# Seven products in place of eight for three of the eight k pairs of gate and up, with the FFN's work in a written-out order

## The chip, the cores and the metric

One core of a Trainium2 chip runs the whole program. The metric is the device time of one execution in microseconds, and the time of a kernel is the median of its runs. All data are float32. One core has a matrix engine (PE, with its weight loads shown as PEld), a vector engine (DVE), a scalar engine (ACT), GpSimd (POOL) and SyncE (SP), which issues most of the transfers.

## The reference

One decoder layer with 256 tokens, D = 2048 channels and a hidden width of 5632. A gated mixer comes first and is the same in both kernels. The change touches the second half of the layer:

```python
def _swiglu(h, w_gate, w_up, w_down):
    return (jax.nn.silu(h @ w_gate) * (h @ w_up)) @ w_down
...
        h = h + _swiglu(_rmsnorm(h, norm_ffn[l]), w_gate[l], w_up[l], w_down[l])
    return _rmsnorm(h, norm_final)
```

## The kernel before, in words

Every matmul operand is held as two rounded parts, hi and lo, so one product of a 128-row weight tile with a block of tokens takes three matmuls: hi by hi, hi by lo, lo by hi (lines 216 to 218 in the token-stationary form "A"). Weights come from DRAM in tiles of 1 MB (`raw`, line 165, three buffers, issued from SP). Each `raw` is split in two halves of 128x1024 elements: ACT casts a half to `hi` (line 175), then DVE subtracts to get `lo` (line 177). There are five pairs of hi/lo buffers, so a split runs some two tiles ahead of PE and then waits for PE to free a buffer.

The work is a list of blocks that `run_blocks` walks. The last stages are four blocks of the mixer's output projection (`out_evac`, lines 702 to 745), then eleven times a gate block and an up block of 512 hidden columns (`ffn_gate_evac`, `ffn_up_evac`), then four blocks of the down projection. In a gate or up block PE goes over 16 k tiles in eight chunks of two; for each chunk it makes the products of both token halves (n = 0, 1). Gate ends in two banks, which ACT reads with silu (line 764); up ends in two banks, which DVE multiplies with that (line 770); the product is transposed on PE (line 777) and split into `hs` (lines 781, 782), which stays in SBUF until the down projection reads it. `out_evac` also makes `y2s` (the normed-gain input of gate and up, split) and the sums of squares, from which `rms` (line 732) makes `r2`, the factor per token.

Tile places the instructions on each engine by priority; `issue_after` and the work queues (`gla_w_`, `conv_w_`) move small work between chunks. Each engine then goes through its own instructions in a fixed order.

A k pair below is two neighbouring k tiles, p = 0 to 7, with gate's and up's 512 columns of one hidden block.

Of the kernel before, what the change touches and what calls it, by code (L numbers as in the profile page):

```python
# [26 lines left out]
NA = 60  # L27
# [7 lines left out]
def trunk(ctx: ExitStack, tc, xT, par, convw, ws, wal2, nfin, out):  # L35
    nc = tc.nc
    cpool = ctx.enter_context(tc.tile_pool(name="cpool", bufs=1))
    apool = ctx.enter_context(tc.tile_pool(name="apool", bufs=NA))
    tpool = ctx.enter_context(tc.tile_pool(name="tpool", bufs=8))
    wpool = ctx.enter_context(tc.tile_pool(name="wpool", bufs=LOOK + 1))  # L40
    pacc = ctx.enter_context(tc.tile_pool(name="pacc", bufs=8, space=bass.MemoryType.PSUM))
# [108 lines left out]
    def load_next():  # L150
        i = nload[0]
        if i >= len(loads):
            return
# [24 lines left out]
        for x in gs:  # L178
            XU.append(atile([P, 2 * T], F32R, "xu"))
            with tc.issue_after(order["a"]), tc.issue_after(order["v"]):  # L180
                split(XU[-1], x)
        staged[i] = (hi, lo)

    def run_blocks():
# [11 lines left out]
        for b in blocks:  # L196
# [38 lines left out]
            group = LOOK if b is blocks[-1] else 1  # L235
            cs = list(range(nch))
            while cs:
                now = cs[:1] if len(cs) > group else cs
                cs = cs[len(now):]
                while nload[0] < len(loads) and nload[0] <= b["first"] + now[0] + LOOK:  # L240
                    load_next()
                for n in range(nt):
                    for c in now:
                        part(c, n)
                for c in now:
                    del staged[b["first"] + c]
                    pump(b["budget"])
# [70 lines left out]
    def x_scaled(k):  # L318
        def f():
            s = atile([P, 2 * T], F32R, "xs")  # L320
# [362 lines left out]
    def pw_evac(blk):  # L683
        def f(n, a):
# [6 lines left out]
            MG[i] = atile([P, 2 * T], F32R, "mgs")  # L691
# [10 lines left out]
    def out_evac(blk):  # L702
        def f(n, a):
# [6 lines left out]
            y = ttile("y2")  # L710
# [4 lines left out]
            if i % 2 == 1:  # L715
                q = atile([P, 2, T], s="hq")
# [6 lines left out]
            if i == 15:  # L723
                def fold():
                    fo = ttile("hf")
                    v.tensor_tensor(fo, sums["h"][:, 0, :], sums["h"][:, 1, :], op=ALU.add)
                    sums["f"] = fo

                def rms():
                    m = misc()  # L730
                    for h in range(2):
                        pe.matmul(m[:, h:h + 1], lhsT=sums["f"][:, h * P:(h + 1) * P], rhs=ones[:, 0:1],
                                  start=True, stop=True)
                    s = cpool.tile([P, 2], F32, tag="r2s", name="r2s")
                    sc.activation(s, m[:, 0:2], AF.Sqrt, bias=eps6)
                    v.reciprocal(r2, s)
                gla_w_.add(0.0, fold)
                gla_w_.add(0.0, rms, 2)
                gla_w_.mark("rstd2")
                for th in range(2):  # L740
                    for nb in range(4):
                        gla_w_.add(0.0, transp(th, nb), 1)
# [16 lines left out]

    def ffn_gate_evac(blk):  # L760
        def f(n, a):
            gla_w_.drain("rstd2")
            GT[n] = tpool.tile([P, NB], F32, tag="gt", name=nm("gt"), bufs=3)
            sc.activation(GT[n], a, AF.Silu, scale=r2[:, n:n + 1])
        return f

    def ffn_up_evac(blk):
        def f(n, a):
            hd = GT[n]
            v.scalar_tensor_tensor(hd, in0=a, scalar=r2[:, n:n + 1], in1=GT[n], op0=ALU.mult, op1=ALU.mult)  # L770
            hs = HS[blk, n] = [atile([P, NB], F32R, "hs") for _ in range(2)]
            st = {}

            def turn():
                st["m"] = m = misc()
                for j in range(4):
                    pe.transpose(m[:, j * P:(j + 1) * P], hd[:, j * P:(j + 1) * P], ident)  # L777

            def cut():
                m = st["m"]  # L780
                sc.copy(hs[0], m)
                v.tensor_tensor(hs[1], m, hs[0].bitcast(F32), op=ALU.subtract)
            gla_w_.add(0.0, turn, 1)
            gla_w_.add(0.0, cut, 1)
            gla_w_.mark(("hs", blk, n))
        return f

    NFT = {}
    HX = []

    def down_before():
        gla_w_.drain(("hs", 10, 1))
        for i in range(HT):
            j = slice(i % 4 * P, (i % 4 + 1) * P)
            HX.append([[t[:, j] for t in HS[i // 4, n]] for n in range(2)])
        for nb in range(4):
            NFT[nb] = atile([P, NB], s="nf")
            nc.sync.dma_start(NFT[nb], nfin[nb * NB:(nb + 1) * NB].partition_broadcast(P))

    def down_evac(nb):  # L800
        def f(n, a):
            h = HTK[n, nb]
            last = nb == 3
            for p, q in ((0, 256), (256, 512)) if last else ((0, 512),):
                v.tensor_tensor(h[:, p:q], a[:, p:q], h[:, p:q], op=ALU.add)
                sq = atile([P, NB], s="dq")
                c = nb + p // 256
                sc.activation(sq[:, p:q], h[:, p:q], AF.Square, accum_out=ss[:, n, c:c + 1])
            if not last:
                v.tensor_tensor(h, h, NFT[nb], op=ALU.mult)  # L810
                if nb == 2 and n == 1:
                    with tc.issue_after(order["a"]):
                        sc.activation(dummy, eps6, AF.Sqrt)
                return
            s1 = cpool.tile([P, 1], F32, tag=f"s1{n}", name=nm("s1"))
            v.reduce_sum(s1, ss[:, n, :], axis=mybir.AxisListType.X)
            s2 = cpool.tile([P, 1], F32, tag=f"s2{n}", name=nm("s2"))
            sc.activation(s2, s1, AF.Sqrt, scale=1.0 / D, bias=eps6)
            s3 = cpool.tile([P, 1], F32, tag=f"s3{n}", name=nm("s3"))
            v.reciprocal(s3, s2)  # L820
            for m in (0, 1, 3, 2):
                o = atile([P, NB], s="fin")
# [54 lines left out]
    for blk in range(11):  # L877
        add_block(NB, KT, "A", lambda: Y2, ffn_gate_evac(blk), budget=0.01)
        add_block(NB, KT, "A", lambda: Y2, ffn_up_evac(blk), budget=0.01)
    for nb in range(4):  # L880
        add_block(NB, HT, "A", lambda: HX, down_evac(nb),
                  before=down_before if nb == 0 else None, budget=0.0)
    run_blocks()


# [57 lines left out]
```

## Time and profile before

| what | value |
|---|---|
| median of three runs | 1681.61 us (1681.47 to 1683.62) |
| the profiled execution's own time | 1683.09 us |
| its span, first to last instruction | 1681.4 us |
| PE busy | 1664.9 us, 8526 matmuls |
| DVE busy | 1150.5 us |
| ACT busy | 857.1 us |
| moved by DMA | 316.35 MB, mean 188 GB/s |

The profiled execution spends 1.7 us outside its span and is 1.5 us above the median. Busy time of PE counts pipelined matmuls, so a PE that is busy all the time may still be slowed inside a stretch. Busy time of DVE and ACT leaves out the time in which the next instruction of the queue waits for another engine.

### The profile page before, as it was taken

Reading aid. Unit: us, or ns where it says so; the run is one execution under the profiler, and the core shown is the slowest. Engines: PE = TensorE matmul, PEld = TensorE weight load, DVE = VectorE, ACT = ScalarE, POOL = GpSimd, SP = SyncE. Lnnn points to the kernel's source line nnn. Section 1 sums busy time; section 2 is a strip of 40 time slices with the busy share of each in tenths; the row PEclk is TensorE's granted clock in tenths of the full one; section 3 lists DMA queues with packets and bytes.
Section 4 is the critical chain, followed back from the end, with each engine's and each line's share of the span. In section 5 each row is a group of like instructions: output and inputs, shape, how many; then the busy total and the mean of one; then the engine's idle time right before and its main releaser. Section 6 shows DMA issues by size and latency. Waiting matters only on the chain.

```text
span 1681.4 us, 21671 instructions
## 1 busy us (share of the span) xinstructions
PE 1664.9 (99%) x8526; PEld 1414.0 (84%) x8526; DVE 1150.5 (68%) x1725; ACT 857.1 (51%) x1161; POOL 4.5 (0%) x10
## 2 busy tenths in 40 slices
PE   9999999999999999999999999999999999999997
PEld 7888888888888888888888888888888888888886
DVE  7898999888888899886777544444444444444453
ACT  6654444666766654584555644444444444444343
POOL 0000000000000000000000000000000000000000
PEclk9999999999999999999999999999999999999999
DMA  8555555555445455545555555555555545655553
GB/s 294 191 198 179 191 185 190 186 183 178 169 172 176 165 187 177 198 177 201 181 217 200 191 188 178 195 178 191 185 191 184 196 180 189 211 198 185 194 200 100
DMA packets 48405, 316.35 MB, mean 188 GB/s; under 512 B 5392, under 2 KB 6672, under 8 KB 11312
## 3 DMA queue, kind: packets, MB, share of 16 engines
q1 hardware_dynamic: 48160, 314.91, 52.7%
q8 instruction: 66, 1.08, 0.3%
q14 instruction: 35, 0.29, 0.0%
q10 hardware_dynamic: 144, 0.07, 0.0%
HBM read 312.86 MB, written 2.10 MB: 187 GB/s over the span
## 4 chain that ended last, share of the span: by engine, by line
PE 97%; DVE 1%; ACT 1%; DMA 1%; issue 0%; ACTq 0%
PE acc L224 31%; PE acc L225 16%; PE acc L216 15%; PE acc L218 15%; PE acc L217 15%; DVE lo L177 1%; ACT hi L175 1%; PE m L777 1%; DVE gt L770 0%; PE m L583 0%; DMA raw<-in_weights_dram 0%; PE m L498 0%; DMA pr<-in_par_dram 0%; PE m L620 0%; PE m L621 0%; PE m L752 0%
## 5 line engine op out<-in xcount | busy, mean ns | idle before, releaser
L177 DVE TENSOR_TENSOR lo<-raw,hi 128x1024 fp32r<-128x1024 f32 (+1 forms) x590 | 717.5, 1217 | 487.5 <-ACT hi L175 485.5
L175 ACT CAST hi<-raw 128x1024 fp32r<-128x1024 f32 (+1 forms) x590 | 617.2, 1047 | 753.1 <-PE acc L218 424.4
L224 PE MATMUL acc<-xs,hi 128*128 128x512 f32 x1280 | 452.4, 398 | 0.0
L225 PE MATMUL acc<-xs,lo 128*128 128x256 f32 x1280 | 359.0, 280 | 0.0
L224 PEld LDWEIGHTS acc<-xs,hi 128*128 128x128 f32 x1280 | 240.3, 188 | 57.8 <-ACT hi L175 0.3
L216 PE MATMUL acc<-hi,y2s 128*128 128x512 f32 x704 | 276.5, 393 | 0.0
L218 PE MATMUL acc<-hi,y2s 128*128 128x512 f32 x704 | 274.3, 390 | 0.0
L217 PE MATMUL acc<-lo,y2s 128*128 128x512 f32 x704 | 274.0, 389 | 0.0
L225 PEld LDWEIGHTS acc<-xs,lo 128*128 128x128 f32 x1280 | 241.8, 189 | 0.1
L380 DVE SCALAR_TENSOR_TENSOR yc<-u,cw,yc 128x255 f32<-128x255 f32 (+14 forms) x480 | 200.1, 466 | 0.1
L218 PEld LDWEIGHTS acc<-hi,y2s 128*128 128x128 f32 x704 | 132.1, 188 | 27.8
L217 PEld LDWEIGHTS acc<-lo,y2s 128*128 128x128 f32 x704 | 132.3, 188 | 26.8
L216 PEld LDWEIGHTS acc<-hi,y2s 128*128 128x128 f32 x704 | 132.2, 188 | 26.6
L216 PE MATMUL acc<-hi,hs 128*128 128x512 f32 x352 | 137.0, 389 | 0.0
L218 PE MATMUL acc<-hi,hs 128*128 128x512 f32 x352 | 136.9, 389 | 0.0
L217 PE MATMUL acc<-lo,hs 128*128 128x512 f32 x352 | 136.9, 389 | 0.0
L224 PE MATMUL acc<-xu,hi 128*128 128x512 f32 x256 | 91.1, 400 | 2.9 <-DVE xu L89 2.9
L224 PE MATMUL acc<-ogs,hi 128*128 128x512 f32 x256 | 89.9, 395 | 0.0
L224 PE MATMUL acc<-us,hi 128*128 128x512 f32 x256 | 88.8, 391 | 0.0
L224 PE MATMUL acc<-mgs,hi 128*128 128x512 f32 x256 | 88.8, 391 | 0.0
L218 PEld LDWEIGHTS acc<-hi,hs 128*128 128x128 f32 x352 | 66.1, 188 | 13.8
L216 PEld LDWEIGHTS acc<-hi,hs 128*128 128x128 f32 x352 | 66.1, 188 | 13.7
(181 smaller groups left out, 1661.3 us busy)
## 6 DMA issues: line engine op xcount, KB each, us to landing
raw<-in_weights_dram SPq DMA_DIRECT2D x289, 1024.0 KB, 4.8
raw<-in_weights_dram SPq DMA_DIRECT2D x8, 256.0 KB, 4.8
raw<-in_weights_dram SPq DMA_DIRECT2D x4, 512.0 KB, 6.5
xr<-in_xT_dram SPq DMA_DIRECT2D x8, 256.0 KB, 5.4
out_dram<-fin SPq DMA_DIRECT2D x8, 256.0 KB, 3.1
x<-in_xT_dram SPq DMA_DIRECT2D x8, 128.0 KB, 4.9
x<-in_xT_dram SPq DMA_DIRECT2D x4, 256.0 KB, 6.8
nf<-in_norm_final_dram SPq DMA_DIRECT2D x4, 256.0 KB, 6.4
```

The costliest lines, as they stand in the source:

```text
L175: order["a"] = sc.copy(fl(hi), r).ins
L177: order["v"] = v.tensor_tensor(fl(lo), r, fl(hi).bitcast(F32), op=ALU.subtract).ins
L216: pe.matmul(a, lhsT=xh, rhs=hi[:, kk, :], start=st, stop=False)
L217: pe.matmul(a, lhsT=xh, rhs=lo[:, kk, :], start=False, stop=False)
L218: last = pe.matmul(a, lhsT=xl, rhs=hi[:, kk, :], start=False, stop=en)
L224: pe.matmul(a, lhsT=wh, rhs=x, start=st, stop=False)
L225: last = pe.matmul(a[:, T:2 * T], lhsT=wl, rhs=xh, start=False, stop=en)
L380: v.scalar_tensor_tensor(y[:, d:T], in0=u_tile(i)[:, 0:T - d], scalar=cw[:, i, CW - 1 - d:CW - d], in1=y[:, d:T], op0=ALU.mult, op1=ALU.add)
L777: pe.transpose(m[:, j * P:(j + 1) * P], hd[:, j * P:(j + 1) * P], ident)
```

## The change

For three of the eight k pairs (p = 2, 5, 7, the list `SEVEN`) the 2x2 block product (two token halves by two k tiles, two k tiles by gate and up) is made with seven products of tiles and sums of tiles in place of eight products; the seven go to seven banks. The other five pairs make eight products into four of these banks (two for the difference of the token halves). The sums of weight tiles are made on DVE as each tile arrives (`t13`, `t2`, `t4`) and split like the others; the sums of token tiles are made once, in `out_evac` (`token_sums`). The seven banks are combined by DVE at a block's end. The FFN is recorded in a written-out order (`keep_in_program_order`), with two running estimates `vt["d"]` and `vt["p"]` that say where the recording puts DVE's and PE's small work. A step is one k pair, with one 1 MB `raw` in two transfers of 512 KB. The split products of hidden blocks 0 to 8 go to DRAM from POOL's queue (`hsd`, 36 transfers of 256 KB) and are loaded again from SP during the first nine steps of the down projection (`hr`, 36 of 256 KB). The down projection takes blocks 9 and 10 first, and makes two blocks of 512 output columns and both token halves at once. SBUF is divided anew: `pers` (16 tiles) holds what lives long, and `apool` and `tpool` give their place to `fpool` and `xpool` when the output projection begins.

```diff
+NPERS = 16
+NF = 38
+NX = 6
+SEVEN = (2, 5, 7)
...
+    def token_sums(p, y):
+        if p in SEVEN:
+            f = atile([P, 4, P], s="sf")
+            v.tensor_tensor(f[:, 0], y[:, 0, H1], y[:, 1, H1], op=ALU.subtract)
+            v.tensor_tensor(f[:, 1], f[:, 0], y[:, 0, H0], op=ALU.subtract)
+            v.tensor_tensor(f[:, 2], y[:, 0, H0], y[:, 0, H1], op=ALU.subtract)
+            v.tensor_tensor(f[:, 3], y[:, 1, H0], f[:, 1], op=ALU.add)
+            SY[p] = [atile([P, 4, P], F32R, "sy") for _ in range(2)]
+            hi, lo = SY[p]
+        else:
+            f = atile([P, 2, P], s="df")
+            v.tensor_tensor(f, y[:, :, H0], y[:, :, H1], op=ALU.subtract)
+            DY[p] = atile([P, 2, 2, P], F32R, "dy")
+            hi, lo = DY[p][:, 0], DY[p][:, 1]
+        sc.copy(hi, f)
+        v.tensor_tensor(lo, f, hi.bitcast(F32), op=ALU.subtract)
+    HORDER = [9, 10] + list(range(9))
...
+        def split_of(src, key):
+            def f():
+                hi, lo = w[key] = wt("hi"), wt("lo")
+                cast(hi, src())
+                sub(lo, src(), hi)
+            return f
+        if kind != "S":
+            ops.append((1.22, split_of(lambda: w["raw"][:, h], h)))
+            return ops
+        def t13():
+            raw = w["raw"]
+            t = w["t"] = xt("t13", F32)
+            fl = raw.rearrange("p a k n -> p (a k) n")
+            kp(v.tensor_tensor(t, fl[:, 0::3], raw[:, 1, 0:1].broadcast_to([P, 2, NB]), op=ALU.add))
+        def s13():
+            hi, lo = w["t13"] = xt("th"), xt("tl")
+            cast(hi, w["t"])
+            sub(lo, w["t"], hi)
+        def t2():
+            raw = w["raw"]
+            kp(v.tensor_tensor(raw[:, 1, 0], w["t"][:, 1], raw[:, 0, 0], op=ALU.add))
+        def t4():
+            raw = w["raw"]
+            kp(v.tensor_tensor(w["t"][:, 0], raw[:, 1, 0], raw[:, 0, 1], op=ALU.add))
+        def s4():
+            t = w["t4"] = xt("t4")
+            cast(t[:, 0], w["t"][:, 0])
+            sub(t[:, 1], w["t"][:, 0], t[:, 0])
+            del w["t"]
+        if h == 0:
+            return ops + [(1.22, split_of(lambda: w["raw"][:, 0], 0)), (1.22, t13), (1.22, s13)]
+        return [(0.66, t2), (1.22, split_of(lambda: w["raw"][:, 1], 1)), (0.66, t4), (0.66, s4)]
...
+        if kind == "P":
+            dd = [[DY[p][:, i, j] for i in range(2)] for j in range(2)]
+            return [(2, [(y_op(k0 + j, 0), half(0, j)) for j in range(2)]),
+                    (4, [(y_op(k0 + j, 1), half(0, j)) for j in range(2)]),
+                    (5, [(y_op(k0 + j, 1), half(1, j)) for j in range(2)]),
+                    (3, [(dd[j], half(1, j)) for j in range(2)])]
+        s = [[t[:, j] for t in SY[p]] for j in range(4)]
+        t4 = [w["t4"][:, 0], w["t4"][:, 1]]
+        return [(1, [(y_op(k0, 0), half(0, 0))]),
+                (6, [(s[1], half(1, 0))]),
+                (7, [(s[2], half("t13", 1))]),
+                (2, [(y_op(k1, 0), half(0, 1))]),
+                (4, [(y_op(k1, 1), t4)]),
+                (5, [(s[0], half("t13", 0))]),
+                (3, [(s[3], half(1, 1))])]
...
+        def b1(a):
+            kp(sc.copy(new("s"), a))
+        def b6(a):
+            tt(new("u2"), a, e["s"])
+        def b7(a):
+            tt(new("u3"), a, e["u2"])
+        def b2(a):
+            tt(e["s"], a, e["s"])
+            silu(e["s"], 0)
+        def b4(a):
+            tt(new("g"), a, e["u3"])
+            silu(e["g"], 1)
+        def b5(a):
+            tt(e["u3"], a, e["u3"], ALU.subtract)
+            tt(e["u2"], a, e["u2"], ALU.subtract)
...
+            kp(v.scalar_tensor_tensor(x, in0=x, scalar=r2[:, n:n + 1], in1=e[g], op0=ALU.mult, op1=ALU.mult))
+            back(blk, n, x)
+        def b3(a):
+            tt(e["u2"], a, e["u2"])
...
+        def cut(m):
+            hi, lo = HSV[blk, n] = ptile(F32R, "hsh"), ptile(F32R, "hsl")
+            cast(hi, m)
+            sub(lo, m, hi)
+            if blk not in HORDER[:2]:
...
+                    nc.gpsimd.dma_start(d[z], q.bitcast(F32))
+        turn(vt["p"] + 1.5, t)
...
+            for z, q in enumerate((hi, lo)):
+                kp(nc.sync.dma_start(q.bitcast(F32), HSD[blk, n][z]))
...
+        for r, (f, c) in enumerate([(h2_norm, 0.25)] + [(h2_turn(th, nb), 0.45) for th in range(2) for nb in range(4)]):
+            turns.append((3.0 + 4.0 * r, c, f))
...
+                if p < 9:
+                    reload(HORDER[2 + p])
```

**DVE and ACT, one pair with seven products.** Before, in the middle of an up block, DVE has one subtraction per half tile, and ACT one cast per half tile (`hs` is the split of the block's gated product):

```order
L177 TENSOR_TENSOR lo_10025<-raw_10022,hi_10024 128x1024
L782 TENSOR_TENSOR hs_9973<-m_10017,hs_9972 128x512
L177 TENSOR_TENSOR lo_10043<-raw_10022,hi_10042 128x1024
L177 TENSOR_TENSOR lo_10061<-raw_10058,hi_10060 128x1024
L177 TENSOR_TENSOR lo_10077<-raw_10058,hi_10076 128x1024
```

In the changed kernel DVE has for the pairs p = 6 and p = 7 of a block (`t_1859` is the sum tile t13, `th` its cast, `t_1864` the split of the sum t4):

```order
L808 TENSOR_TENSOR lo_9986<-raw_9982,hi_9985 128x1024
L808 TENSOR_TENSOR lo_9999<-raw_9982,hi_9998 128x1024
L808 TENSOR_TENSOR lo_10009<-raw_10005,hi_10008 128x1024
L842 TENSOR_TENSOR t_1859_10018<-raw_10005 128x1024
L808 TENSOR_TENSOR tl_10027<-t_1859_10018,th_10026 128x1024
L851 TENSOR_TENSOR raw_10005<-t_1859_10018,raw_10005 128x512
L808 TENSOR_TENSOR lo_10041<-raw_10005,hi_10040 128x1024
L855 TENSOR_TENSOR t_1859_10018<-raw_10005 128x512
L808 TENSOR_TENSOR t_1864_10051<-t_1859_10018,t_1864_10051 128x512
```

and ACT has for them:

```order
L805 CAST hi_9998<-raw_9982 128x1024
L805 CAST hi_10008<-raw_10005 128x1024
L805 CAST th_10026<-t_1859_10018 128x1024
L805 CAST hi_10040<-raw_10005 128x1024
L805 CAST t_1864_10051<-t_1859_10018 128x512
L805 CAST hi_10063<-raw_10060 128x1024
```

Three of a pair's casts (`th`, `hi_10040`, `t_1864`) read what DVE has written just before, and the DVE instruction that follows reads that cast.

**PE, the first gate block.** Before, the two matmuls for `r2` (line 732) stand in the fifth chunk, behind 55 matmuls of the block:

```order
L216 MATMUL acc_9332<-hi_9328,y2s_9058 128x512
L217 MATMUL acc_9332<-lo_9329,y2s_9058 128x512
L218 MATMUL acc_9332<-hi_9328,y2s_9058 128x512
L216 MATMUL acc_9339<-hi_9328,y2s_9044 128x512
L732 MATMUL m_9362<-ones,hf_9324 128x1 x2
```

In the changed kernel they stand behind the third of the first pair's four groups (18 matmuls after the first of gate and up):

```order
L1139 MATMUL m_9399<-hi_9258,y2s_8620 128x512
L1140 MATMUL m_9399<-lo_9259,y2s_8620 128x512
L1141 MATMUL m_9399<-hi_9258,y2s_8620 128x512
L1034 MATMUL m_9406<-ones,hf_9383 128x1 x2
L1139 MATMUL m_9411<-hi_9258,dy_8625 128x512
```

They moved forward; `hf` is the last thing that `out_evac` makes.

**SP, the end of gate and up.** Before, SP issues one 1 MB tile after the other, with the four loads of the final norm's factor among them:

```order
L165 DMA raw_12732<-in_weights_dram 128x2048
L165 DMA raw_12766<-in_weights_dram 128x2048
L798 DMA nf_12688<-in_norm_final_dram 128x512
L798 DMA nf_12690<-in_norm_final_dram 128x512
L798 DMA nf_12692<-in_norm_final_dram 128x512
L798 DMA nf_12694<-in_norm_final_dram 128x512
L165 DMA raw_12800<-in_weights_dram 128x2048
```

In the changed kernel four loads of a block's stored products stand ahead of each tile, nine times (the first here):

```order
L823 DMA raw_13238<-in_weights_dram 128x1024 x2
L1116 DMA nf_13269<-in_norm_final_dram 128x512 x2
L1116 DMA nf_13272<-in_norm_final_dram 128x512 x2
L1028 DMA hr_13275<-hsd_9854 128x512
L1028 DMA hr_13276<-hsd_9854 128x512
L1028 DMA hr_13279<-hsd_9841 128x512
L1028 DMA hr_13280<-hsd_9841 128x512
L823 DMA raw_13320<-in_weights_dram 128x1024 x2
```

The queue now moves twice the bytes per step during those nine steps.

## Rows read from the trace of the kernel before

**Rows 1.** The page: busy times, and the chain that ended last by engine.
```profile
PE 1664.9 (99%) x8526; PEld 1414.0 (84%) x8526; DVE 1150.5 (68%) x1725; ACT 857.1 (51%) x1161; POOL 4.5 (0%) x10
...
PE 97%; DVE 1%; ACT 1%; DMA 1%; issue 0%; ACTq 0%
```

**Rows 2.** Busy time by stretch: us, engines' busy (count), granted clock, DMA share, GB/s.
```profile
933.00:1433.30 500.30, 496.38 (x2239) 407.89 (x2238) 249.69 (x239) 221.14 (x240) 0.00 (x0) 1.00 0.52 185
1023.50:1068.50 45.00, 44.65 (x201) 36.75 (x200) 22.13 (x20) 19.17 (x20) 0.00 (x0) 1.00 0.53 187
1433.30:1672.50 239.20, 239.20 (x1058) 198.14 (x1056) 113.24 (x104) 96.04 (x106) 0.00 (x0) 1.00 0.51 182
```

**Rows 3.** Groups of one gate and up block (1068.5 to 1113.5): busy, mean ns | idle before.
```profile
L177 DVE TENSOR_TENSOR lo<-raw,hi 128x1024 fp32r<-128x1024 f32 x16 | 19.6, 1225 | 22.9 <-ACT hi L175 22.9
L175 ACT CAST hi<-raw 128x1024 fp32r<-128x1024 f32 x16 | 16.9, 1053 | 24.9 <-PE acc L218 24.9
...
L770 DVE SCALAR_TENSOR_TENSOR gt<-acc,r,gt 128x512 f32<-128x512 f32 x2 | 1.4, 742 | 0.0
L782 DVE TENSOR_TENSOR hs<-m,hs 128x512 fp32r<-128x512 f32 x2 | 1.4, 684 | 0.0
```

**Rows 4.** PE in order of time: start, us; the first and last of 18 starts.
```profile
1089.80 0.39 PE L216 MATMUL acc<-hi,y2s 128*128 128x512 f32 x1
...
1093.65 0.39 PE L218 MATMUL acc<-hi,y2s 128*128 128x512 f32 x1
```

**Rows 5.** The chain at the end of the last up block: start, us, what.
```profile
1432.87 0.66 PE m L777 x4
```

**Rows 6.** Groups of the whole program on DVE, 512 wide, one operand broadcast.
```profile
L434 DVE TENSOR_TENSOR yc<-yc,lnrs 128x512 f32<-128x512 f32 x8 | 5.4, 688 | 0.0
```

**Rows 7.** Groups of the whole program on ACT, casts 512 wide.
```profile
L175 ACT CAST hi<-raw 128x512 fp32r<-128x512 f32 x8 | 5.0, 620 | 5.0 <-DMA raw<-in_weights_dram 4.9
```

**Rows 8.** DVE in order of time: start, us [idle before <-releaser].
```profile
916.47 0.69 DVE L720 TENSOR_TENSOR hss<-hss,hq 128x512 f32<-128x512 f32 x1
917.07 0.42 DVE L257 TENSOR_TENSOR mt<-acc,ms 128x256 f32<-128x256 f32 x1
917.52 0.42 DVE L709 TENSOR_TENSOR h<-mt,xr 128x256 f32<-128x256 f32 x1
...
941.29 0.35 DVE L711 TENSOR_SCALAR y<-h,pr 128x256 f32<-128x256 f32 x1
...
945.37 0.42 DVE L726 TENSOR_TENSOR hf<-hss 128x256 f32<-128x256 f32 x1
...
947.00 0.17 DVE L736 RECIPROCAL r<-r2s 128x2 f32<-128x2 f32 x1
...
1101.29 1.23 DVE L177 TENSOR_TENSOR lo<-raw,hi 128x1024 fp32r<-128x1024 f32 x1 [1.50 <-ACT hi L175]
...
1114.88 1.23 DVE L177 TENSOR_TENSOR lo<-raw,hi 128x1024 fp32r<-128x1024 f32 x1 [1.50 <-ACT hi L175]
1116.03 1.41 DVE L770 SCALAR_TENSOR_TENSOR gt<-acc,r,gt 128x512 f32<-128x512 f32 x2
```

**Rows 9.** ACT in order of time.
```profile
941.67 0.41 ACT L88 CAST y2s<-y 128x256 fp32r<-128x256 f32 x1 [1.45 <-DVE y L711]
...
946.71 0.26 ACT L735 ACTIVATE r2s<-m,eps 128x2 f32<-128x2 f32 x1
...
1100.20 1.05 ACT L175 CAST hi<-raw 128x1024 fp32r<-128x1024 f32 x1 [1.67 <-PE acc L218]
```

**Rows 10.** Busy time by stretch, at the start, at the down projection's start, and at the end.
```profile
15.00:20.00 5.00, 4.03 (x24) 3.23 (x22) 3.55 (x8) 2.94 (x6) 0.00 (x0) 1.00 0.98 372
...
1433.30:1438.00 4.70, 4.70 (x24) 3.88 (x22) 2.69 (x4) 1.83 (x3) 0.00 (x0) 1.00 0.95 300
...
1674.00:1679.00 5.00, 0.00 (x0) 0.00 (x0) 1.47 (x4) 1.96 (x5) 0.00 (x0) 0.82 0.57 189
1676.00:1681.00 5.00, 0.00 (x0) 0.00 (x0) 0.23 (x1) 0.42 (x1) 0.00 (x0) 0.62 0.64 210
```

More of the change, by code (lines that the diff above doesn't have):

```diff
@@ L233, in part @@
                     b["evac"](n, acc.pop(n))
[L235 to L240, printed above, removed]
+            for c in range(nch):
+                while nload[0] + halves[0] <= b["first"] + c + LOOK:
                     load_next()
                 for n in range(nt):
[L243 to L247, printed above, removed]
+                    part(c, n)
+                del staged[b["first"] + c]
+                pump(b["budget"])
     def merged_sum(a, bias=None):
@@ L723, in f @@
             if i == 15:
[L724 to L736, printed above, removed]
@@ new lines, in trunk, with next_prep, half_ahead, y_op @@
+    todo = deque()
+    def next_prep():
+        while not todo:
+            if halves[0] >= 2 * len(steps):
+                return False
+            todo.extend(half_ops(halves[0]))
+            halves[0] += 1
+        cost, f = todo.popleft()
+        f()
+        vt["d"] += cost
+        return True
+    def half_ahead():
+        if todo:
+            return
+        next_prep()
+        while todo:
+            next_prep()
+    def y_op(k, t):
+        return [Y2[k][:, i * T + t * P:i * T + (t + 1) * P] for i in range(2)]
@@ new lines, in products @@
+    def products(i):
+        what, b, p, kind = steps[i]
+        w = prepared[i]
+        half = lambda key, j: [t[:, j] for t in w[key]]
+        if what == "dn":
+            hb = HORDER[p // 2]
+            out = []
+            for t in range(2):
+                for n in range(2):
+                    prs = []
+                    for j in range(2):
+                        jj = slice((p % 2 * 2 + j) * P, (p % 2 * 2 + j + 1) * P)
+                        prs.append(([x[:, jj] for x in HSV[hb, t]], half(n, j)))
+                    out.append(((t, n), prs))
+            return out
+        k0, k1 = 2 * p, 2 * p + 1
+        if kind == "P":
[13 more added lines that the diff above has]
+                (3, [(s[3], half(1, 1))])]
@@ new lines, in reload, with h2_norm @@
+    def reload(blk):
+        for n in range(2):
+            if blk == 8:
+                h = xt("hr")
+                hi, lo = h[:, 0], h[:, 1]
+            else:
+                hi, lo = (atile([P, NB], F32R, "hr") for _ in range(2))
+            for z, q in enumerate((hi, lo)):
+                kp(nc.sync.dma_start(q.bitcast(F32), HSD[blk, n][z]))
+            HSV[blk, n] = (hi, lo)
+    def h2_norm():
+        m = misc()
+        for h in range(2):
+            kp(pe.matmul(m[:, h:h + 1], lhsT=sums["f"][:, h * P:(h + 1) * P], rhs=ones[:, 0:1],
+                         start=True, stop=True))
+        s = cpool.tile([P, 2], F32, tag="r2s", name="r2s")
+        kp(sc.activation(s, m[:, 0:2], AF.Sqrt, bias=eps6))
+        later(0.2, lambda: kp(v.reciprocal(r2, s)), 0.5)
@@ L767, in ffn_up_evac @@
[L767 to L785, printed above, removed]
+                kp(pe.transpose(m[:, q * P:(q + 1) * P], H2[i // 2][:, i % 2, th * P:(th + 1) * P], ident))
@@ L786, in ffn_up_evac @@
+            HTK[th, nb] = ptile(s="htk")
+            kp(sc.copy(HTK[th, nb], m))
         return f
     NFT = {}
[L789 to L798, printed above, removed]
@@ L876, in trunk @@
         add_block(NB, KT, "M", lambda: MG, out_evac(blk), before=out_before(blk))
[L877 to L882, printed above, removed]
+    g0[0] = sum(b["nk"] * b["width"] for b in blocks) // (4 * NB)
     run_blocks()
+    run_ffn()
 def kernel(**inputs):
```

254 lines of the change are left out of this document (203 added, 51 removed).

## The prediction

> **What bounds the kernel now.** I read the page's busy times and its chain first. PE is busy 99% of the span and the chain runs 97% through PE [rows 1], so before the change time is PE time. Next come the stretches: gate and up take 500.3 us, one block of them 45.0 us, the down projection 239.2 us [rows 2]. In a block DVE is busy 22.1 us and ACT 19.2 us. The groups of one block say why they idle: DVE's 16 subtractions wait 22.9 us for ACT's casts, and those wait 24.9 us for PE to free a buffer [rows 3]. Today these waits are behind PE and cost nothing. The point for this change is their form: a subtraction can't begin before its cast ends, and what stands behind it on DVE waits too.
>
> **The change, part by part.** *PE.* Starts lie 3.85 us apart over 17 steps, 0.2265 us for a matmul [rows 4], 0.68 us for a product of three. Three pairs save a product in each of 11 blocks: 33 products, 22.4 us. A block then has 61 products, 41.5 us, and two groups of four transposes of 0.66 us, 1.3 us [rows 5]: 42.8 us.
>
> *DVE's prices.* A subtraction of 128x1024 takes 1.23 us [rows 3]; when the next needs no wait, that starts 1.15 us after it (1114.88 to 1116.03 [rows 8]). An instruction 512 wide takes 0.69 us, also with a broadcast operand [rows 6], and reading a bank (684 ns [rows 3]); the next starts after 0.60 us (916.47 to 917.07), or 0.03 us after its end if it reads its result (917.07, 0.42 us, to 917.52 [rows 8]). A sum of weight tiles is not in this trace. It reads two tiles and writes one like a subtraction, so I take the subtraction's price; its bounds are the 1.15 us above and twice 0.69 us.
>
> *The hand-over to ACT and back.* ACT starts 0.03 us after DVE ends (941.29 plus 0.35, to 941.67), its cast takes 1.05 us, and DVE starts 0.04 us after (1100.20 plus 1.05, to 1101.29) [rows 8, 9]: DVE stands for 1.12 us. For a cast 512 wide, 0.62 us [rows 7], it is 0.69 us.
>
> *A pair with seven products on DVE*, in the order shown: the first split's subtraction 1.15; the sum t13 1.23 and a stand of 1.12 for its cast; subtraction 1.15; t2 0.69 and a stand of 1.12, since the cast of up's half reads what t2 wrote; subtraction 1.15; t4 0.69 and a stand of 0.69; its subtraction and the start of the next pair's cast behind t4's, 1.00. Sum 10.0 us, 3.2 us of it standing. Nothing on DVE can fill it: the next instruction in its queue is the one that waits.
>
> *A block on DVE.* Three such pairs 30.0; five pairs with eight products, two subtractions each, 11.5; the bank reads, seven of 0.60 and two products of some 0.66 (742 ns less the overlap [rows 3]), with 0.3 for three that read the one before, 5.8; two hsl subtractions 1.2. **48.5 us, against PE's 42.8 and today's 45.0.** So DVE sets the pace. Buffers can't help: a lead of two steps is used up once, and each block loses it again. ACT has some 24 us of work per block, spread, and follows.
>
> *The first block.* The output projection's last bank reads now have no splits between them (five of 1.15 us went), but they gain the token sums: for the last two pairs one difference and its split (0.42 each) and four small sums with a split of 0.69, about 2.6 us, and some 3 us of stands for ACT's casts, which the splits had covered. So `hf` ends about when it did, 12.8 us into the stretch (945.79 against 933.0 [rows 2, 8]). But PE's matmuls for r2 now stand behind 18 others, 4.3 us into it: PE waits some 8.5 us. DVE goes on after the two matmuls (an estimate of 0.3), square root 0.26, reciprocal 0.17, a cast and the hand-overs [rows 8, 9], at 14.7 us. Then three pairs of 10.0 and three of 2.3 us, 36.9, and PE's last three products, 2.0, less 0.3 of the last pair's hand-over: the block ends at 53.3 us. Ten more at 48.5 make 538.3. Behind the first down step PE waits for the last block's bank reads (9.6 us after DVE's last split of gate and up, where PE is there at 7.5) and transposes: 3.4 us. The stretch is 541.7 us, against 500.3: **41.4 us more**.
>
> *What hides.* The earlier token sums (two pairs in each of three output blocks, some 2.5 us of DVE per block) go into DVE's stands for casts, 1.5 us where a split has nothing beside it [rows 8]; without that cover they cost up to 7 us. Nobody waits soon for the 36 stores on POOL's queue; they share the transfer engines, at 0.52 busy [rows 2]. Issuing 512 KB twice for 1 MB keeps the bytes.
>
> *The down projection* has the same 1056 matmuls and splits. New is that SP's queue moves 2.1 MB in each of nine steps of 5.44 us, 385 GB/s. The rows give 372 GB/s at 0.98 busy and 300 GB/s at 0.95 [rows 10]. With the norm's 1 MB ahead, the tile for the eleventh step lands 53.6 or 66.5 us after gate and up end and is wanted at about 55: between 0 and 12 us late. I take 3, nearer the faster row, whose pieces are also mixed. The Trainium skill, DMA: Bandwidth & Descriptors, section Bandwidth, gives 341 GB/s for 1 MB transfers and advises transfers of 1 MB or more; by that figure, an estimate, the tile would be 3.1 us late and the sum the same, while the advice speaks against the loads of 256 KB. No row here shows such loads beside full tiles for nine steps.
>
> *The end* has the same last instructions. I take nothing, with 1 us either way.
>
> **Sum.** 41.4 + 3.0 = 44.4 us on the profiled execution's own 1683.1, 1727.5 us. That execution lies 1.5 us over the median: I predict **1726.0 us**.
>
> **Rivals.** *A, faster: the casts hide.* If 4.0 of the 9.6 us that DVE stands in a block were filled, the kernel would equal the one before; with 5.7 us or more filled, PE sets the pace. Then 11 blocks of 42.8, the wait of 8.5, eight groups of transposes of H2 at up to 0.66 and 0.2 at the start make 484.8, 15.5 less than today, and with 3 for the down projection the median would be 1669.1 us. For it: today DVE stands 22.9 us per block and PE never notices [rows 3], and the written estimates of DVE's time come to 40 us per block. Against it: these estimates have no stand in them, and the order puts each subtraction directly behind the instruction whose result it needs a cast of. 0.10, and 0.02 for a draw. *B, slower by the queue:* the down projection at 300 GB/s, 9 us more than the sum, 1735 us; 0.12. For it: 385 GB/s is more than any row. Against it: two tiles are loaded ahead and lag grows slowly. *C, slower by the clock:* PE stands once for 8 us, and 5.7 us of each block, most of it at p = 2, just after the bank reads. In the last 5 us the granted clock is 0.62, with PE done [rows 10]: on its way from 2.4 to 1.2 GHz. If PE came back from the 8 us at 1.2 GHz and did the next ten products so, they would take 6.8 us more; PE is nearly the bound in that block, and 5 us would reach the end: 1731 us, 0.08. The Trainium skill, TensorE: Matmul & The Clock Gate, Part 1, says that idle PE falls to half clock and that work releases it. The tail row agrees with the first half; no row shows it after a short stand in the middle. That PE would not get fewer products can be left out: the order has 99 matmuls less.
>
> **How the numbers follow.** The forecast, DVE setting the pace with no extra, has 0.68. A block of 47.5 to 50.0 us moves it by -10 and +15, the first block by 5 either way, the transfers by -3 and +9. Rivals B and C lie inside that. The range 1700 to 1746 leaves out A and the draw, 0.12, part of half-hidden stands, 0.03, and 0.05 above. A measurement here tells 0.2%, 3.4 us, from nothing. Faster 0.10, same 0.02, slower 0.88.
>
> **What would show it.** Right: blocks 48 to 49 us long from the second on; DVE's `tl`, the second `lo` and t4's split waiting 1.1, 1.1 and 0.7 us for ACT, 33 times each; PE idle some 6 us per block, most of it at p = 2 for `lo` and before the transposes; one PE wait of 8 us for `hf`. Wrong: blocks of 43 us with PE never idle (A), DVE waiting for tiles in the down projection's first ten steps by more than 5 us (B), a granted clock under 0.9 in gate and up (C), or DVE sums far from 1.2 us.

## The result and the profile after

| what | before | changed |
|---|---|---|
| median, measured side by side (4 runs each) | 1681.54 us (1681.08 to 1683.62) | 1732.31 us (1730.89 to 1734.69) |
| ratio, 95% interval | | 1.0301, 1.0283 to 1.0319 |
| profiled execution, own time | 1683.09 us | 1732.18 us |
| forecast | | 1726.0 us, 1700 to 1746 |

The kernel is slower, as forecast: by 3.0%, and 6.3 us more than the point of the forecast. The page of the changed kernel, busy times and the chain by engine, beside [rows 1]:

```profile
PE 1668.6 (96%) x8427; PEld 1406.2 (81%) x8427; DVE 1340.0 (77%) x1992; ACT 907.4 (52%) x1246; POOL 23.9 (1%) x46
...
PE 77%; DVE 12%; ACT 5%; issue 4%; DMA 1%; ACTq 0%; SPq 0%; DVEq 0%
```

PE has its 99 matmuls fewer, and the chain that was 97% PE now runs a fifth of its way through DVE, ACT and time for which the profile shows no wait ("issue"). Stretches of the changed kernel (us, busy of PE, PEld, DVE, ACT, POOL with counts, granted clock, DMA share, GB/s): gate and up, two single blocks of it, the down projection, the tail.

```profile
932.80:1479.00 546.20, 496.77 (x2132) 397.12 (x2131) 424.81 (x476) 264.90 (x314) 19.49 (x36) 0.97 0.55 188
1037.20:1086.20 49.00, 44.85 (x193) 36.08 (x192) 38.54 (x43) 23.29 (x28) 2.15 (x4) 0.97 0.57 193
1086.20:1135.20 49.00, 44.18 (x194) 35.24 (x193) 38.56 (x43) 23.32 (x28) 2.15 (x4) 1.00 0.56 193
1479.00:1721.30 242.30, 240.74 (x1065) 198.71 (x1063) 122.09 (x116) 99.87 (x111) 0.00 (x0) 1.00 0.62 217
1721.30:1730.20 8.90, 0.13 (x1) 0.00 (x0) 2.30 (x7) 2.54 (x7) 0.00 (x0) 0.66 0.50 165
```

Against [rows 2] gate and up grew by 45.9 us (500.3 to 546.2) and the down projection by 3.1 (239.2 to 242.3). All of the loss is there. A block takes 49.0 us, was 45.0; DVE is busy for 38.5 of them and stands for 10.5. The groups of the first of these two blocks on DVE, and the casts of weights on ACT, show what they stand for (busy, mean ns | idle before), beside [rows 3]:

```profile
L808 DVE TENSOR_TENSOR lo<-raw,hi 128x1024 fp32r<-128x1024 f32 x17 | 20.2, 1222 | 4.9 <-ACT hi L805 4.8
L808 DVE TENSOR_TENSOR tl<-t,th 128x1024 fp32r<-128x1024 f32 x3 | 3.7, 1225 | 3.4 <-ACT th L805 3.4
L842 DVE TENSOR_TENSOR t<-raw 128x1024 f32<-128x1024 f32 x3 | 3.6, 1217 | 0.0
L808 DVE TENSOR_TENSOR t<-t,t 128x512 fp32r<-128x512 f32 x3 | 2.1, 693 | 2.1 <-ACT t L805 2.1
L805 ACT CAST hi<-raw 128x1024 fp32r<-128x1024 f32 x17 | 17.1, 1047 | 7.0 <-DVE raw L851 4.0 <-issue 2.2 <-PE m L1141 0.8
```

4.9, 3.4 and 2.1 us add up to 10.4: nearly all that DVE stands in this block is for casts. In [rows 3] it stood for casts too, 22.9 us, but those casts were themselves waiting for PE (24.9 us); now the casts of weights wait 0.8 us for PE in the block and 4.0 us for the sum `t2` that DVE makes (L851). One pair with seven products (p = 5 of this block) on DVE in order of time:

```profile
1057.47 5.88 DVE L808 TENSOR_TENSOR lo<-raw,hi 128x1024 fp32r<-128x1024 f32 x5 [0.25 <-ACT hi L805]
1063.27 1.22 DVE L842 TENSOR_TENSOR t<-raw 128x1024 f32<-128x1024 f32 x1
1065.60 1.23 DVE L808 TENSOR_TENSOR tl<-t,th 128x1024 fp32r<-128x1024 f32 x1 [1.11 <-ACT th L805]
1066.74 0.68 DVE L851 TENSOR_TENSOR raw<-t,raw 128x512 f32<-128x512 f32 x1
1068.68 1.22 DVE L808 TENSOR_TENSOR lo<-raw,hi 128x1024 fp32r<-128x1024 f32 x1 [1.25 <-ACT hi L805]
1069.82 0.68 DVE L855 TENSOR_TENSOR t<-raw 128x512 f32<-128x512 f32 x1
1071.19 0.69 DVE L808 TENSOR_TENSOR t<-t,t 128x512 fp32r<-128x512 f32 x1 [0.69 <-ACT t L805]
1072.14 1.22 DVE L808 TENSOR_TENSOR lo<-raw,hi 128x1024 fp32r<-128x1024 f32 x1 [0.26 <-ACT hi L805]
```

The last of the five `lo` of the first row is this pair's own first subtraction; it begins 1.23 before 1063.35, at 1062.12. From there to the next pair's split at 1072.14 is 10.0 us, of which 3.3 are the four stands in brackets. Over the whole stretch and the last bank reads behind it (932.8 to 1488) DVE's waits for casts of gate and up are (us, times, longest):

```profile
DVE lo L808 <- ACT hi L805: 53.7, 79, 1.5
DVE tl L808 <- ACT th L805: 36.9, 33, 1.1
DVE t L808 <- ACT t L805: 23.5, 33, 0.8
```

### The profile page after: what moved, and what is told of

Its sections match the earlier page's. It is cut to its first block, busy times and chain, and to the rows that moved or that the text cites. A ratio compares the mean times of both kernels' runs of the same rounds, so it can differ in the third digit from the quotient of the medians.

```text
span 1730.2 us, 22362 instructions
## 1 busy us (share of the span) xinstructions
PE 1668.6 (96%) x8427; PEld 1406.2 (81%) x8427; DVE 1340.0 (77%) x1992; ACT 907.4 (52%) x1246; POOL 23.9 (1%) x46
## 4 chain that ended last, share of the span: by engine, by line
PE 77%; DVE 12%; ACT 5%; issue 4%; DMA 1%; ACTq 0%; SPq 0%; DVEq 0%
PE acc L240 31%; PE acc L241 16%; PE m L1140 8%; PE m L1141 8%; PE m L1139 8%; DVE lo L808 6%; ACT hi L805 3%; DVE u L953 2%; PE acc L232 2%; PE acc L234 2%; PE acc L233 2%; DVE t L842 1%; ACT th L805 1%; DVE tl L808 1%; DVE u L981 1%
## 5 line engine op out<-in xcount | busy, mean ns | idle before, releaser
L191 ACT CAST hi<-raw 128x1024 fp32r<-128x1024 f32 (+1 forms) x326 | 339.0, 1041 | 343.4 <-PE acc L240 285.9
L193 DVE TENSOR_TENSOR lo<-raw,hi 128x1024 fp32r<-128x1024 f32 (+1 forms) x326 | 393.4, 1207 | 112.4 <-ACT hi L191 110.8
L808 DVE TENSOR_TENSOR lo<-raw,hi 128x1024 fp32r<-128x1024 f32 x264 | 315.4, 1222 | 168.2 <-ACT hi L805 162.9
L805 ACT CAST hi<-raw 128x1024 fp32r<-128x1024 f32 x264 | 268.7, 1049 | 200.1 <-PE m L1141 128.8
L1139 PE MATMUL m<-hi,y2s 128*128 128x512 f32 x396 | 159.1, 402 | 0.0
L1140 PE MATMUL m<-lo,y2s 128*128 128x512 f32 x396 | 156.4, 395 | 0.0
L1141 PE MATMUL m<-hi,y2s 128*128 128x512 f32 x396 | 156.0, 394 | 0.0
L1139 PE MATMUL m<-hi,hr 128*128 128x512 f32 x288 | 112.1, 389 | 0.0
L1140 PE MATMUL m<-lo,hr 128*128 128x512 f32 x288 | 112.1, 389 | 0.0
L1141 PE MATMUL m<-hi,hr 128*128 128x512 f32 x288 | 112.1, 389 | 0.0
L1139 PEld LDWEIGHTS m<-hi,y2s 128*128 128x128 f32 x396 | 76.0, 192 | 17.0 <-issue 1.5
L1141 PEld LDWEIGHTS m<-hi,y2s 128*128 128x128 f32 x396 | 75.7, 191 | 16.4
L1140 PEld LDWEIGHTS m<-lo,y2s 128*128 128x128 f32 x396 | 76.2, 192 | 15.4
```

What stands on the lines that cost most here:

```text
L805: kp(sc.copy(dst, src))
L808: kp(v.tensor_tensor(dst, src, hi.bitcast(F32), op=ALU.subtract))
L1139: kp(pe.matmul(a, lhsT=xh, rhs=wh, start=st, stop=False))
L1140: kp(pe.matmul(a, lhsT=xh, rhs=wl, start=False, stop=False))
L1141: kp(pe.matmul(a, lhsT=xl, rhs=wh, start=False, stop=en))
```

## The experiments

The theory: DVE goes through its queue in order, a pair with seven products makes it stand three times for a cast of what it has just written, and with three such pairs its column of work is longer than PE's. The rivals: the added sums are too much work by themselves; PE loses its time on its own, by the wait for the norm or a lower clock; the written order or the detour through DRAM is the price. The kernel before had a median of 1683.06 us beside the first four runs and 1682.89 us beside the last three, so the ratios are what compares.

**The order within a pair (e_fill).** The same numbers of instructions on PE, DVE and ACT as in the changed kernel (8427, 1992 and 1246), in another order.

```diff
+        def a():
+            w[0] = wt("hi"), wt("lo")
+            cast(w[0][0], w["raw"][:, 0])
...
+            kp(v.tensor_tensor(t, fl[:, 0::3], w["raw"][:, 1, 0:1].broadcast_to([P, 2, NB]), op=ALU.add))
+        def b():
+            w["t13"] = xt("th"), xt("tl")
+            cast(w["t13"][0], w["t"])
+            kp(v.tensor_tensor(w["raw"][:, 1, 0], w["t"][:, 1], w["raw"][:, 0, 0], op=ALU.add))
+        def c():
+            sub(w[0][1], w["raw"][:, 0], w[0][0])
+        def d():
+            w[1] = wt("hi"), wt("lo")
+            cast(w[1][0], w["raw"][:, 1])
+            sub(w["t13"][1], w["t"], w["t13"][0])
+        def e_():
+            kp(v.tensor_tensor(w["t"][:, 0], w["raw"][:, 1, 0], w["raw"][:, 0, 1], op=ALU.add))
+        def f_():
+            t = w["t4"] = xt("t4")
+            cast(t[:, 0], w["t"][:, 0])
+            sub(w[1][1], w["raw"][:, 1], w[1][0])
+        def g_():
+            t = w["t4"]
+            sub(t[:, 1], w["t"][:, 0], t[:, 0])
...
-            return ops + [(1.22, split_of(lambda: w["raw"][:, 0], 0)), (1.22, t13), (1.22, s13)]
-        return [(0.66, t2), (1.22, split_of(lambda: w["raw"][:, 1], 1)), (0.66, t4), (0.66, s4)]
+            return ops + [(1.22, a), (0.66, b), (1.22, c)]
+        return [(1.22, d), (0.66, e_), (1.22, f_), (0.66, g_)]
```

> The same instructions as the changed kernel, in another order: within a pair with seven products DVE makes t13, t2, the first half's subtraction, tl, t4, the second half's subtraction and t4's split, and ACT casts the first half, th, the second half, t4, so that something else always stands between a sum and the subtraction that needs its cast. Theory (DVE stands some 10 us per block for casts, and these stands set the block): a pair falls from 10 to 6.5 us on DVE, a block's DVE column from 49.0 to about 38.7 us, under PE's 42.8; blocks of 42.8 to 44 us, the stretch of gate and up some 482 to 494 us in place of 546.2, the kernel 1668 to 1681 us. Rival 1 (the added arithmetic, not the standing, is the price): 1729 to 1735 us, as the changed kernel. Rival 2 (PE loses its time by itself, by the lower clock after it stood and the wait for the norm): the 8 us wait and a clock of 0.97 stay, and the gain is under 15 us.

Measured: 1685.59 us, ratio 1.0017 (1.0008 to 1.0026). Of the loss of 3.0% all but 0.2% is gone with the order alone, so the sums were not its price: they are all still there. A pair on DVE in order of time in e_fill:

```profile
1099.09 1.23 DVE L843 TENSOR_TENSOR t<-raw 128x1024 f32<-128x1024 f32 x1 [0.56 <-DMA raw<-in_weights_dram]
1100.35 0.69 DVE L848 TENSOR_TENSOR raw<-t,raw 128x512 f32<-128x512 f32 x1
1100.96 1.22 DVE L808 TENSOR_TENSOR lo<-raw,hi 128x1024 fp32r<-128x1024 f32 x1
1102.10 1.22 DVE L808 TENSOR_TENSOR tl<-t,th 128x1024 fp32r<-128x1024 f32 x1
1103.35 0.69 DVE L859 TENSOR_TENSOR t<-raw 128x512 f32<-128x512 f32 x1
1103.96 1.22 DVE L808 TENSOR_TENSOR lo<-raw,hi 128x1024 fp32r<-128x1024 f32 x1
1105.09 0.68 DVE L808 TENSOR_TENSOR t<-t,t 128x512 fp32r<-128x512 f32 x1
1105.69 2.46 DVE L808 TENSOR_TENSOR lo<-raw,hi 128x1024 fp32r<-128x1024 f32 x2
```

It takes 6.6 us (1099.09 to 1105.69) in place of 10.0, with no stand for a cast in it (its one wait, 0.56 us, is for a weight tile). Yet the time lies 4.6 us over the top of what was expected. One block (columns as above), and the one wait of PE in the block behind it, in order of time:

```profile
1032.75:1077.10 44.35, 43.05 (x192) 35.00 (x191) 38.16 (x43) 23.32 (x28) 2.13 (x4) 1.00 0.62 214
```

```profile
1093.45 0.50 PE L1148 MATMUL m<-lo,sy 128*128 128x512 f32 x1 [1.28 <-DVE lo L808]
```

DVE's busy time is what it was (38.2 us against 38.5), but it no longer sets the block. The reading is that the block is 44.35 us because PE stands at p = 2 for the second subtraction, and that PE, with its wait of 8.2 us for the norm, sets the first block now. Both are put to the test below (e_fill357 and e_best).

**The norm later (e_late).** Only the place of the norm's matmuls, in the changed kernel.

```diff
-            turns.append((3.0 + 4.0 * r, c, f))
+            turns.append((14.0 + 4.0 * r, c, f))
```

> The changed kernel with the norm's two matmuls (and the transposes of H2 behind them) put 11 us later in the recorded order, behind some 16 more products. Theory: PE's 8.2 us wait for hf goes, but the first block ends by DVE, which begins the third pair's splits when the output projection's work is done, so PE stands at the third pair instead; DVE saves only the 1.5 us in which it waits for the square root and some of the late cast behind it: 0 to 3 us gained, 1729 to 1732 us. Rival (the PE wait is on the path): 8 us gained, 1724 us. Against both: if the transposes of H2 now fall where PE has no slack, some of it is lost.

Measured: 1731.60 us, ratio 1.0288 (1.0273 to 1.0304): from the changed kernel's 1.0301 nothing that the intervals tell apart. PE in order of time in the first block of e_late, the rows with a wait:

```profile
944.66 0.49 PE L1139 MATMUL m<-hi,y2s 128*128 128x512 f32 x1 [0.81 <-ACT hi L805]
946.32 0.50 PE L1140 MATMUL m<-lo,y2s 128*128 128x512 f32 x1 [1.16 <-DVE lo L808]
951.51 0.79 PE L1139 MATMUL m<-hi,sy 128*128 128x512 f32 x1 [4.46 <-ACT hi L805]
952.76 0.80 PE L1140 MATMUL m<-lo,sy 128*128 128x512 f32 x1 [0.47 <-DVE lo L808]
```

The one wait of 8.2 us became four of 6.9 us in all, at p = 2. While DVE sets the pace of a block, as here, where PE waits in it does not matter.

**Fewer pairs (e_two, e_none).**

```diff
-SEVEN = (2, 5, 7)
+SEVEN = (2, 5)
```

> Seven products for two pairs (p = 2, 5) in place of three. Theory: a block on DVE is 49.0 less 7.7 (10.0 for a pair with seven products, 2.3 for one with eight), 41.3 us, now under PE's 62 products and transposes, 43.5 us: PE sets the pace nearly always, blocks of 43.5 to 45 us, first block some 50 us, stretch 486 to 500 us, the kernel 1672 to 1686 us. So with one pair fewer it is faster by 46 to 60 us although PE has 7.5 us more to do. Rival (the written order or the DRAM detour cost, and the pairs gain): 1740 us.

e_none has `SEVEN = ()` and bank reads for four banks:

```diff
+        def done0(b, a):
...
+            if b == 2:
+                later(0.0, lambda: g("s", a, 0))
+            elif b == 4:
+                later(0.0, lambda: g("g", a, 1))
+            elif b == 5:
+                later(0.66, up1)
+            else:
+                later(0.66, up0)
+                later(0.66, lambda: gated("u3", "g", 1))
+                later(0.66, lambda: gated("u2", "s", 0))
+        if not SEVEN:
+            return done0
```

> No pair with seven products: all eight pairs make eight products into four banks, with the written order, the DRAM detour and the new SBUF layout kept; ACT reads two banks with silu and DVE the two others. Theory: PE sets the pace with 64 products and transposes, 44.9 us per block, and the only price of the written order is the 8.2 us wait at the norm: stretch 494 plus 8 to 11, the kernel 1687 to 1692 us, that is 6 to 10 us over the kernel before. Rival (the written order, the transfers through DRAM or the new layout are the price): 1725 us and above.

Measured: e_two 1671.20 us, ratio 0.9928 (0.9911 to 0.9944); e_none 1685.82 us, ratio 1.0018 (1.0009 to 1.0028). Each lies about 1 us under the range that was expected. A block of e_none, and then of e_two:

```profile
1037.39:1081.81 44.42, 44.42 (x202) 36.87 (x200) 23.42 (x23) 19.00 (x20) 2.15 (x4) 1.00 0.64 213
```

```profile
1037.38:1080.44 43.06, 43.06 (x196) 35.76 (x195) 34.31 (x38) 22.16 (x25) 2.14 (x4) 1.00 0.64 220
```

PE is never idle in either. From none to two pairs a block falls by 1.36 us, twice the 0.68 of a product: here each pair gives all that it promises. The third takes DVE past PE, and the block jumps from 43.06 to 49.0. The written order, the new layout and the detour through DRAM together, which e_none keeps, cost 0.2%. That is a balance: PE waits 7.0 us for `hf` in e_none (8.2 had been expected), and its blocks are 44.42 us against 45.0 in [rows 2]. With the changed order in place of fewer pairs e_fill comes to the same time as e_none: what the three pairs save (11 times three products, 22 us) and what they still cost, most of it by the stands at p = 2, are equal there by chance.

**One stand of three (e_fill1).** The changed kernel with only the first half's subtraction moved behind t13.

```diff
+        def s0():
+            w[0] = wt("hi"), wt("lo")
+            cast(w[0][0], w["raw"][:, 0])
         def s13():
             hi, lo = w["t13"] = xt("th"), xt("tl")
             cast(hi, w["t"])
+            sub(w[0][1], w["raw"][:, 0], w[0][0])
             sub(lo, w["t"], hi)
...
-            return ops + [(1.22, split_of(lambda: w["raw"][:, 0], 0)), (1.22, t13), (1.22, s13)]
+            return ops + [(0.0, s0), (1.22, t13), (2.44, s13)]
```

> The changed kernel with one of a pair's three stands filled: the first half's subtraction is made behind t13 in place of ahead of it, while ACT casts th; everything else in the old order. Theory: tl's wait of 1.12 us goes, 33 times, and DVE still sets the pace (49.0 less 3.4 is 45.6 us, against 42.4 that PE needs), so the kernel gains 11 times 3.4, 37 us: 1692 to 1699 us, blocks of 45.5 to 46 us, and the two other waits stay. Rival (PE's own loss at p = 2 or its clock sets the block): under 10 us gained.

Measured: 1699.15 us, ratio 1.0098 (1.0081 to 1.0114). A block of e_fill1, and DVE's waits in one (1033 to 1079):

```profile
1041.98:1087.58 45.60, 43.42 (x193) 35.01 (x192) 38.51 (x43) 23.39 (x27) 2.16 (x4) 1.00 0.60 208
```

```profile
DVE lo L808 <- ACT hi L805: 5.7, 8, 1.2
DVE t L808 <- ACT t L805: 2.1, 3, 0.8
```

The wait of `tl` is gone from the list, the two others are there, and the block is 45.60 us: 3.4 us less, three stands of 1.12. The ten blocks from the second on together fall by 32.9 us (458.8 against 491.6). DVE's busy time is the same 38.5. That is the theory's term, measured by itself. The kernel gained 33 us, not 37 (0.2 us over the expected range), because eleven blocks had been counted and the first gained nothing: neither a shorter wait of PE (e_late) nor a shorter column of DVE alone (here) shortens that one, so the two are about level in it. From PE's first matmul of gate and up to the row of three `u` reads at the first block's end are 58.9 us in the changed kernel, 58.6 in e_late and 59.3 in e_fill1; in e_best below, where both are shortened, they are 51.7.

**The pairs one step later, and the norm too (e_fill357, e_best).** Both on e_fill:

```diff
-SEVEN = (2, 5, 7)
+SEVEN = (3, 5, 7)
```

> As e_fill, with the pairs p = 3, 5, 7 in place of 2, 5, 7, so that a pair with eight products stands between the bank reads at a block's end and the first pair with seven. Theory: the 2.0 us by which e_fill's blocks (44.35) lie above three products under those of e_none (44.42 less 2.04 is 42.38) are PE's wait at p = 2, 1.28 us for the second subtraction and what goes with it, because DVE comes from 6.1 us of bank reads to 5.5 us of work ahead of that subtraction; a step later the lead has been made up: blocks of 42.4 to 42.9 us, the kernel 1664 to 1672 us. Rival (DVE has too little slack per block wherever the pairs stand): the wait moves to p = 3 and the kernel stays within 5 us of e_fill's 1685.6.

and in e_best beside that

```diff
-            turns.append((3.0 + 4.0 * r, c, f))
+            turns.append((14.0 + 4.0 * r, c, f))
```

> As e_fill357, with the norm's matmuls 11 us later in the recorded order. Theory: now that PE sets the pace, its 8.2 us wait for hf and the slow products behind it are on the path, as they were not in e_late: most goes, some 2 to 4 us of standing stay at p = 2, which DVE prepares only after hf: 5 to 9 us under e_fill357, 1657 to 1666 us. Rival (as in e_late, the wait only moves): within 2 us of e_fill357.

Measured: e_fill357 1669.86 us, ratio 0.9925 (0.9910 to 0.9940); e_best 1661.11 us, ratio 0.9875 (0.9860 to 0.9889). A block of e_fill357, and PE's waits in the whole of gate and up and the down projection of e_best:

```profile
1038.93:1081.71 42.78, 42.78 (x193) 35.08 (x192) 38.16 (x43) 23.52 (x28) 2.17 (x4) 1.00 0.65 221
```

```profile
PE m L1148 <- DVE lo L808: 1.2, 1, 1.2
PE m L1147 <- ACT hi L805: 0.8, 1, 0.8
```

The block is 42.78 us with PE busy throughout: 61 products and the transposes, the 42.8 us worked out from [rows 4, 5]. That is 0.28 us less than with two pairs, where a product is 0.68: the row of the eight transposes is 1.32 us long here (1038.93) and 1.03 us in e_two (1037.38), which is 0.29 of the missing 0.40. And the edit that gave nothing in e_late gives 8.7 us here, because the path has gone back to PE. The profiled executions are 9.0 us apart: 7.1 us are in the first block (58.8 to 51.7), and 2.6 us lie ahead of gate and up, in code that the edit does not touch. e_best beats the kernel before by 1.25% and the changed kernel by 4.1% (0.9875 over 1.0301).

## Why the prediction was right, point by point

**The mechanism.** DVE sets the pace by standing for its own casts: right. `tl`, the second `lo` and t4's split wait 1.12 (36.9 over 33 times), 1.1 to 1.3 and 0.71 us (23.5 over 33 times), forecast 1.1, 1.1 and 0.7. The sum tile t13 takes 1.22 us, priced as a subtraction at 1.23. A pair takes 10.0 us, as summed. That the stands and not the work decide is shown by e_fill1 and e_fill: with one of the three filled the block falls by what that one measures, with all three it falls until PE stops it.

**The block: 49.0, forecast 48.5.** The step that was undersized is the bank reads, summed at 5.8 us, and what follows them. Bank reads run from 1039.13 to 1045.23 in one block, 6.1 us. And the second split of p = 0 begins 1.42 us after the first (1084.52 to 1085.94), not 1.15, since its cast stands on ACT behind the copy of the first bank, which the sum left out. ACT in order of time, and the subtraction that waits:

```profile
1084.39 0.57 ACT L959 COPY s<-m 128x512 f32<-128x512 f32 x1
1084.86 2.00 ACT L805 CAST hi<-raw 128x1024 fp32r<-128x1024 f32 x2
```

```profile
1085.94 1.23 DVE L808 TENSOR_TENSOR lo<-raw,hi 128x1024 fp32r<-128x1024 f32 x1 [0.20 <-ACT hi L805]
```

From the first block's bank reads (`u` at 991.69) to the last block's (1483.33) are ten blocks, 491.6 us, against 485: 6.6 us, of which 1.2 are the clock in the second block (below) and most of the rest these half microseconds.

**The first block.** `hf` ends 12.4 us into the stretch (12.8), PE waits 8.2 us for it (8.5), DVE's first split begins at 14.8 (14.7). DVE in order of time:

```profile
944.75 0.42 DVE L743 TENSOR_TENSOR hf<-hss 128x256 f32<-128x256 f32 x1
946.63 0.17 DVE L1038 RECIPROCAL r<-r2s 128x2 f32<-128x2 f32 x1 [1.46 <-ACT r2s L1037]
947.56 1.23 DVE L808 TENSOR_TENSOR lo<-raw,hi 128x1024 fp32r<-128x1024 f32 x1 [0.77 <-ACT hi L805]
```

The stretch less the ten blocks leaves 54.6 us for the first, against 53.3. The prediction had put this wait into PE's path in rival A alone and let DVE set the block in the forecast; e_late shows that this was right, and e_fill1 that it was a near thing.

**The down projection.** Here a term was wrong: 3 us were taken for tiles that come late, and PE waited for none: one cast on ACT waited for its tile, 0.4 us. The stretch is 242.3 us, 239.2 and the 3.1 us of the last block's transposes and the wait for its bank reads (forecast 3.4, counted with gate and up). In the first steps the transfers moved (us, engines, clock, DMA share, GB/s)

```profile
1489.00:1530.00 41.00, 41.00 (x183) 33.95 (x182) 20.62 (x19) 15.12 (x16) 0.00 (x0) 1.00 1.01 378
```

378 GB/s over 41 us, with loads of 256 and 512 KB mixed, and PE was busy throughout. Of [rows 10] the row with 372 GB/s foretold this, and the one with 300, rival B, did not. The figure of the Trainium skill, DMA: Bandwidth & Descriptors, section Bandwidth (341 GB/s for transfers of 1 MB, there issued from GpSimd), was too low for this stretch, whose loads SP issues. Its advice to make transfers of 1 MB or more could be ignored here at no cost.

**The sum.** Gate and up and the down projection together came to 788.5 us against the forecast 783.9 (541.7 and 242.2), so 4.6 us more: 6.6 in the ten blocks, 1.3 in the first, less 3.0 for the transfers and 0.3 at the last bank reads. That the 3.0 us for tiles that did not come late made up for part of the rest is luck. The profiled execution took 1732.18 us against 1727.5. The other 1.6 us of the 6.3 is the correction to the median: the execution of before lay 1.5 us over its median, and that of the changed kernel lies 0.1 under.

**The rivals.** A fell: DVE's 10.5 us of standing in a block were filled by nothing. What A would have given for filled stands was 1669.1 us with blocks of 42.8; e_fill357, which fills them by its order and has the first pair a step later, has 42.78 and 1669.86 (the blocks are the reading that counts; A's sum for the kernel also holds the 3 us for late tiles). B fell with the row above. C was there, much smaller. After the 8.2 us wait PE came back at 1.2 GHz: the granted clock is 0.50 from 945 to 949. PE in order of time, the norm's matmuls and the first ones behind them (rows between left out are 0.43 us apart, then 0.24):

```profile
945.32 0.98 PE L1034 MATMUL m<-ones,hf 128*128 128x1 f32 x4 [8.21 <-DVE hf L743]
...
946.73 0.63 PE L1140 MATMUL m<-lo,dy 128*128 128x512 f32 x1
947.16 0.63 PE L1141 MATMUL m<-hi,dy 128*128 128x512 f32 x1
...
949.54 0.40 PE L1141 MATMUL m<-hi,y2s 128*128 128x512 f32 x1
949.78 0.40 PE L1139 MATMUL m<-hi,y2s 128*128 128x512 f32 x1
```

So it lost 1.4 us (seven matmuls at 0.43 in place of 0.23), not the 6.8 that were worked out for ten products, in a block that DVE sets anyway. That PE falls to half clock when idle and that work releases it, as the Trainium skill says in TensorE: Matmul & The Clock Gate, Part 1, agrees with these rows. In the second block, behind stands of 1.87 and 0.55 us at p = 2, twelve matmuls in a row start 0.43 us apart (granted clock 0.52 from 1005 to 1011), and that did reach DVE: ACT waits for PE to free a buffer, and DVE for ACT.

```profile
1011.96 1.05 ACT L805 CAST hi<-raw 128x1024 fp32r<-128x1024 f32 x1 [1.88 <-PE m L1141]
```

```profile
1013.04 1.23 DVE L808 TENSOR_TENSOR lo<-raw,hi 128x1024 fp32r<-128x1024 f32 x1 [1.15 <-ACT hi L805]
```

This block is 50.2 us long (991.69 to 1041.91), the others 49.0 to 49.3. The two blocks in the first table show that the clock is otherwise no part of the loss: one has 0.97 and the other 1.00, and both take 49.0 us.

**What was over- or undersaid.** PE's idle time was forecast at 6 us per block. In the block with the clock at 1.00 it is 4.8 us (49.0 less 44.2): 1.8 and 0.8 at p = 2, 0.7 at p = 7 and 1.6 before the transposes. Most of it is at the places named. The other 1.4 us are in the busy time, which counts pipelined matmuls: the same products and transposes without a stand are 42.8 us (e_fill357), 6.2 less than 49.0.

## What to carry to other kernels

A product saved on the bounding engine was paid for on another here: sum that engine's column with its stands, not its busy time, and compare it with what the bounding engine then needs. In a queue that runs in order, an instruction that needs a round trip through another engine should have other work of at least the trip's length (here 1.12 us) ahead of it; the same instructions in another order were worth 47 us. An edit that moves a wait can be worth nothing while the wait is off the path (the later norm: 0) and most of its length once it is on it (7.1 us of the first block), so fixes are tried again when the bound has changed.

## What the runs showed that was not expected

The same two stands of PE at p = 2 (1.84 and 0.76 us, ending at 1054.04 and 1055.30, and again at 1103.12 and 1104.38) were followed by matmuls 0.43 us apart in the first of the two blocks above (granted clock 0.97) and not in the second (1.00). The stands ahead of them were the same, so what makes the clock fall in one block and not in the next stays open. Nor does it keep to a place in the program: in e_late the second block has 1.00, and the fourth, behind the same two stands, has 0.93 and takes 50.4 us. Transfers of 256 KB and 512 KB mixed ran at 378 GB/s for 41 us, more than either row of [rows 10]. And in e_fill t13 waits for its weight tile in seven of the eleven blocks, 0.56 us in the pair shown and 1.8 us at most: no subtraction stands ahead of it any more. It costs nothing in that place: PE stands once per block, at p = 2, and this is at p = 5 each time.
